# Moving the first block's rows to the scratch ring, the roots to the attention's banks, and spreading four weight sums

## The chip, the cores and the metric

The kernel runs on one core of one Trainium2 chip. The metric is the device time of one execution in microseconds (us). A core has five engines that this text names as the profile does: PE (TensorE, matmuls; PEld is its weight load), DVE (VectorE), ACT (ScalarE), POOL (GpSimd) and SP (SyncE, which here issues nearly all DMAs). Each works through its own queue of instructions, and they wait for one another by semaphores.

## The reference, cut to what matters

One layer of a streaming encoder over 2048 tokens of width 1024, with chunked softmax attention (16 heads of 64; a chunk of 64 frames reads itself and the 8 chunks before it) and a SwiGLU FFN of inner width 2816. Every sub-layer is normed before and after:

```python
def rms_norm(x, g):
    y = x * lax.rsqrt(jnp.mean(x * x, axis=-1, keepdims=True) + RMS_EPS)
    return y * g

h = rms_norm(x, g_pre_mix)
m = chunk_relpos_attention(h, w_qkv, w_o, rel_bias)   # softmax(q k / 8 + bias) v, then @ w_o
x = x + rms_norm(m, g_post_mix)
h = rms_norm(x, g_pre_ffn)
x = x + rms_norm((silu(h @ w_gate) * (h @ w_up)) @ w_down, g_post_ffn)
```

All of it is in float32. The kernel splits each factor of a dense product in a high and a low part and adds three products (`products`, lines 195 to 199; a triple of matmuls below).

## The kernel before, in words

The tokens lie along the free axis: a tile is 128 features by 512 tokens, and 8 such tiles (`KT`) make a quarter of the sequence (`NQ` = 4), two quarters a group (`NG` = 2). The work comes in four stages:

- `project()` (line 1320) makes values, queries and keys, group by group, and writes them to DRAM. The dense products go by a Strassen-like scheme of seven block products (`BLOCKS`, line 39) instead of eight, for which sums of four weight blocks, S1 to S4, are needed. `block_items` (line 894) builds them for group 0: it loads four raw blocks, and `make(n)`, called a few products ahead of the use of product n, splits the block for PE (ACT copies the high part, DVE subtracts for the low part, lines 130 to 132). After some of the products it calls `sum_`, which adds two raw blocks in place on DVE (line 905) and stores the sum by a DMA of POOL's queue (line 906), for group 1 to read. The values call it with `early=False`, the queries and keys (`w_qk`) and the gate and up weights (`w_gu`) with `early=True`.
- The attention runs in 128 slots of 128 queries (lines 1582 to 1610), eight pairs of heads for each of the quarters 1, 0, 2, 3 (`SEQ_OF`). In a slot PE transposes the probabilities (`transposed`, `fifth`), computes the scores of three slots ahead (`scores`), and every fourth slot multiplies by the values (`output`, whose high part is copied by ACT and whose low part by DVE in the function that it returns, `low`). PSUM banks: `ring` holds two banks, from slot 32 on three (`later_banks`), which the transposes and the output take in turn (`turn_of`, line 474); the scores have banks of their own; two banks of tag `mm` serve the rest.
- Beside a quarter of the attention runs the o-projection of the quarter before (`o_quarter`, line 609): eight output tiles of eight triples each, each tile in an `mm` bank, then copied by ACT to an `io` tile (lines 628, 629), stored to DRAM, and squared into the sum of its norm (line 631). `fill` (line 1552) hands out these triples over the slots, and for each of them `tick` gives one credit to the list `later`, whose steps run as their costs are covered.
- From the second of these quarters on (`n > 0`, line 1592) `later` holds the end of the quarter before: `Late.rows` turns the sum of squares into a row of roots (`rstd_steps`, line 267: eight small matmuls into a bank of `norm_bank`, a power on POOL, and after a pause four transposes into another such bank), `Late.write` norms the eight tiles, adds the residual on POOL and stores x1, and `Blocks.sums` (line 642) loads the eight tiles of x1 again, squares them on ACT, adds the squares on DVE into `total`, and takes the root for the norm before the FFN. `behind` (line 219) makes such a list of n loads and uses: step k issues load k and then use k - lag, and each step costs w n / (n + lag).
- The FFN: `gate_up` and `down`, group by group, on the same scheme of seven products.

Buffers that the change touches: the `io` ring of three tiles (line 249) holds the copies of the o-projection (`y`), the residuals of `Late.write` (`res`) and the rows of `Blocks.sums` (`sum`); the scratch ring (`scratch`, `narrow`, lines 238 to 247) has four tiles in the attention and holds the y tiles of `Late.write`, squares, and more in other stages. Only PE's order is written by hand (line 1531); the order of the instructions on the other engines and of SP's DMAs is made by the Tile scheduler when the program is built. All tiles of a ring are given out as they come free.

Of the kernel before, what the change touches and what calls it, by code (L numbers as in the profile page):

```python
# [13 lines left out]
ALU = mybir.AluOpType  # L14
# [9 lines left out]
KT = D // P  # L24
# [14 lines left out]
BLOCKS = ("B11", "B21", "T1", "T2", "B22", "T3", "T4")  # L39
# [10 lines left out]
def trunk(  # L50
# [14 lines left out]
    pe, act, dve, pool = nc.tensor, nc.scalar, nc.vector, nc.gpsimd  # L65
# [137 lines left out]
    later = deque()  # L203
# [15 lines left out]
    def behind(w, n, lag, load, use):  # L219


        def one(k):
            def go():
                if k < n:
                    load(k)
                if k >= lag:
                    use(k - lag)

            return w * n / (n + lag), go

        return [one(k) for k in range(n + lag)]

    def pause(w):
        return [(w, lambda: None)]
# [3 lines left out]
    def scratch(name):  # L238

        n = turn[0] % (4 + phase.get("tmp", 0))  # L240
        turn[0] += 1
        if n >= 4:
            return phase["fp"].tile([P, HALF], F32, tag="tmp", name=name, bufs=phase["tmp"])
        return xp.tile([P, HALF], F32, tag="sc", name=name, bufs=4)

    def narrow(name):
        return scratch(name)[:, :HALF]

    def io(name):
        return xp.tile([P, HALF], F32, tag="io", name=name, bufs=3)  # L250
# [4 lines left out]
    def nrm_tile(name):  # L255
        return row_tile("nrm", name)

    def add_square(src, total, first, eng=dve, sq=None):
        if first:
            act.activation(total, src, AF.Square)  # L260
            return
        if sq is None:
            sq = scratch("sq")[:, : src.shape[-1]]
        act.activation(sq, src, AF.Square)
        eng.tensor_tensor(total, total, sq, op=ALU.add)

    def rstd_steps(total, dst, wait=8.0, keep=None, bank=None, extra=None, then=None):

        nb = total.shape[-1] // P
        bank = bank or norm_bank
        r = {}

        def by_token():
            pt = bank("pssq")
            for b in range(nb):
                terms = [total] if extra is None else [total, extra]  # L280
                for n, t in enumerate(terms):
                    pe.matmul(
                        pt[:, 0, b : b + 1], t[:, b * P : b * P + P], ones[:, 0:1],
                        start=n == 0, stop=n == len(terms) - 1,
                    )
            m = const.tile([P, 4], F32, tag="ms", name="ms", bufs=2)
            dve.tensor_scalar(m[:, :nb], pt[:, 0, :nb], 1.0 / D, EPS, op0=ALU.mult, op1=ALU.add)  # L287
            r[0] = const.tile([P, 4], F32, tag="rs", name="rs", bufs=2) if keep is None else keep
            pool.tensor_tensor(r[0][:, :nb], m[:, :nb], neg_half.to_broadcast([P, nb]), op=ALU.pow)  # L289

        def back():
            if then is None:
                spread(r[0], dst, bank)
            else:
                then(transposed(r[0], nb, bank))

        return [(1.0, by_token)] + pause(wait) + [(1.0, back)]
# [39 lines left out]
        return [(w, f) for f in steps]  # L337

    def norm_bank(name):
        return ps.tile([P, 4, P], F32, tag="mm", name=name)  # L340

    def spread(r, dst, bank=norm_bank):
# [56 lines left out]
    phase = {}  # L399
# [45 lines left out]
    turn_of = [1]  # L445
    st_of, ring = [], []
# [11 lines left out]
    class Attend:  # L458
# [9 lines left out]
        def bank(self, name):  # L468

            if self.alone and name != "t5":  # L470
                return ps.tile([P, HALF], F32, tag="mm", name="tt")
            if self.alone:
                return ring[0]
            turn_of[0] += 1
            return ring[turn_of[0] % 3]
# [157 lines left out]
    class Blocks:  # L633
# [8 lines left out]
        def sums(self, w, on_all=False, which=range(2)):  # L642

            steps = []
            if on_all:
                self.rows = []
            for t in which:
                c = {}

                def load(k, t=t, c=c):  # L650
                    c[k] = io("sum")
                    sp.dma_start(c[k], self.src[t][:, k, :])

                def use(k, c=c):
                    if k == 0 and on_all:
                        self.total = phase["fp"].tile([P, HALF], F32, tag="tot", name="row", bufs=2)
                        self.rows.append(self.total)
                    elif k == 0:
                        self.total = nrm_tile("total")
                    add_square(c.pop(k), self.total, k == 0)  # L660

                steps += behind(w, KT, 2, load, use)
                if on_all:
                    steps.append((0.0, lambda t=t: later.extendleft(reversed(root_steps(self.rows[t], 1.5)))))
                    continue
                steps.append((5.0, lambda t=t: rstd_steps(self.total, None, keep=self.r[t])[0][1]()))
            return steps

        def spreads(self):
# [224 lines left out]
    def block_items(src, key, early=True, ahead=None):  # L894

        r = {}
        sums_d[key] = {a: dram.tile([P, 1024], F32, name=f"s_{key}_{a}") for a in ("S1", "S2", "S3", "S4")}

        def fetch_(names):
            for a in names:  # L900
                r[a] = phase["fp"].tile([P, 1024], F32, tag="w4", name="raw4", bufs=phase["w4"])
                sp.dma_start(r[a], src[BLOCK_AT[a]])

        def sum_(name, to, a, b, op=ALU.add):
            dve.tensor_tensor(r[to], r[a], r[b], op=op)
            last_pool[0] = pool.dma_start(sums_d[key][name], r[to])

        def make(n):
            w = w_tile(f"w{key}_{n}")
            a = FACTOR[n]  # L910
            split_part(*w, r[{"S1": "A21", "S2": "A11", "S4": "A12", "S3": "A21"}.get(a, a)])
            if n == ("B11" if early else "B21"):
                sum_("S1", "A21", "A21", "A22")
                sum_("S2", "A11", "A11", "A21")
            if n == "B21":
                sum_("S4", "A12", "A12", "A11")
            if n == "T2":
                sum_("S3", "A21", "A11", "A22", ALU.subtract)
            return w

        at = {"B11": ("A11", "A12"), "B21": ("A21", "A22")}
        if not early:
            at = {"B11": ("A11",), "B21": ("A12",), "T1": ("A21", "A22")}
        ahead = ahead or {}
        return [
            (lambda n=n: fetch_(at.get(n, ())), lambda _, n=n: make(n), *ahead.get(n, (6, 3))) for n in BLOCKS
        ]
# [227 lines left out]
    class Late:  # L1155
# [27 lines left out]

            return [(0.0, go)]

        def write(self, w, eng=dve):
            c = {}

            def load(dt):
                c[dt] = y, res = narrow("y"), io("res")  # L1190
                sp.dma_start(y, self.y[:, dt, :])
                sp.dma_start(res, self.res[:, dt, :])

            def use(dt):
                y, res = c.pop(dt)
                dve.scalar_tensor_tensor(
                    y, y, gt[:, self.gain, dt : dt + 1], self.total, op0=ALU.mult, op1=ALU.mult
                )
                eng.tensor_tensor(y, res, y, op=ALU.add)
                sp.dma_start(self.dst[:, dt, :], y)  # L1200

            return behind(w, KT, 2, load, use)


    rs, rows_of = [], {}
# [329 lines left out]
    sums_, done = weight_sums(), 0.0  # L1535
# [46 lines left out]
    for t in range(slots):  # L1582
        share = left[0] / max(per - t % per - 1, 1)
        if t > 0 and t % 4 == 0:
            fill(0.5 * share)
            low = jobs[t // 4 - 1].output()
            if t % per == 0:
                n = t // per - 1
                fill(1e9)
                drain()  # L1590
                work, left[0] = o_quarter(SEQ_OF[n]), KT * KT * 3 * C512
                if n > 0:
                    late = lates[SEQ_OF[n - 1]]
                    later.extend(late.rows(4.0) + late.write(3.0, pool))
                    later.extend(blocks[0].sums(2.0, which=[SEQ_OF[n - 1]]))
        if t == 16:
            fetch()
        elif t in (20, 22):
            part_split(t // 2 - 10)
        job = jobs[t // 4]  # L1600
        job.transposed(t % 4)
        if t + AHEAD - 1 < slots:
            jobs[(t + AHEAD - 1) // 4].scaled()
        ahead(t + AHEAD)
        if t > 0 and t % 4 == 0:
            low()
        fill(0.5 * share)
        job.fifth()
        if t % 4 < 3:
            fill(0.5 * share)  # L1610
# [96 lines left out]
```

## Time and profile before

| | |
|---|---|
| median of three runs | 2392.41 us (2391.65 to 2392.60) |
| the profiled execution | 2390.56 us, its span 2388.8 us |
| busy: PE, DVE, ACT, POOL | 98%, 68%, 48%, 13% of the span |
| first matmul of the o-projection's four quarters | 617.7, 729.4, 905.8, 1061.6 us |
| mean granted clock of TensorE | 0.993 |

The profile lists each instruction of the profiled execution with its start and duration, by line of the kernel. A tile's name stands before the arrow for what is written and behind it for what is read, as in `y<-mm`. In brackets stands the idle time of the engine before an instruction and what ended it. Matmuls overlap on PE, so the mean duration of one (about 0.39 us for 512 columns) is longer than the distance between two (0.22 us). The granted clock is 1 at full speed and 0.5 at half.

### The profile page before, as it was taken

The numbers are of one execution on the slowest core, as the hardware profiler recorded it, in microseconds if no ns is written. First come the engines' busy times: TensorE is split into PE (matmuls) and PEld (weight loads), VectorE is DVE, ScalarE is ACT, GpSimd is POOL, SyncE is SP. The second block draws the span as 40 slices with busy tenths as digits, with TensorE's granted clock in tenths as the row PEclk, the third lists the DMA queues.
The fourth block names the chain that finished last, engine by engine and source line by source line (L and its number), as shares of the span: only waits on it lengthen the run. The fifth ranks groups of instructions, "written<-read, shape, count | busy, mean of one in ns | idle before, by whom it ended". The sixth has DMA issues, their size and how long they took to land.

```text
span 2388.8 us, 32904 instructions
## 1 busy us (share of the span) xinstructions
PE 2330.5 (98%) x11456; PEld 1907.9 (80%) x11456; DVE 1635.1 (68%) x2618; ACT 1145.4 (48%) x2015; POOL 319.0 (13%) x422
## 2 busy tenths in 40 slices
PE   8999999989999989999999999999999999999998
PEld 6878788878777767778888888888888888888886
DVE  8776856666566666659777777687657676545577
ACT  6544543367666656656333332365443333334454
POOL 1021010034334434420000000000000000000001
PEclk9999999999999989999999999999999999999999
DMA  8799988688897988846776553577666657447664
GB/s 309 256 292 329 297 263 261 181 235 225 220 257 207 291 228 241 258 169 204 245 246 210 181 185 131 175 236 256 215 207 205 216 161 234 150 154 247 192 193 144
DMA packets 230358, 531.81 MB, mean 223 GB/s; under 512 B 26384, under 2 KB 42784, under 8 KB 225712
## 3 DMA queue, kind: packets, MB, share of 16 engines
q1 hardware_dynamic: 218288, 482.52, 63.8%
q0 software_dynamic: 11904, 47.19, 6.8%
q8 instruction: 90, 1.47, 0.2%
q14 instruction: 76, 0.62, 0.1%
HBM read 382.23 MB, written 170.44 MB: 231 GB/s over the span
## 4 chain that ended last, share of the span: by engine, by line
PE 68%; DVE 3%; ACT 1%; issue 1%; DMA 1%; POOL 0%; DVEq 0%; SPq 0%; ACTq 0%
PE pd L197 6%; PE pd L199 6%; PE pd L198 6%; PE pb L197 5%; PE pb L198 5%; PE pb L199 5%; PE tt L600 4%; PE pa L198 3%; PE pa L197 3%; PE pa L199 3%; PE pc L197 3%; PE pc L198 3%; PE pc L199 3%; PE tt L570 3%; PE mm L197 2%; PE mm L199 2%
## 5 line engine op out<-in xcount | busy, mean ns | idle before, releaser
L555 POOL TENSOR_SCALAR sc<-sc,rows 128x640 f32<-128x640 f32 (+4 forms) x256 | 194.5, 772 | 313.0 <-DVE rows L552 134.1
L543 ACT ACTIVATE sc<-sc,rows 128x640 f32<-128x640 f32 (+4 forms) x256 | 193.2, 757 | 72.5 <-DVE rows L539 71.4
L197 PE MATMUL pb<-hb,w_wg_T 128*128 128x512 f32 x528 | 206.0, 390 | 3.2 <-DVE terms L1012 3.2
L199 PE MATMUL pb<-hb,w_wg_T 128*128 128x512 f32 x528 | 205.5, 389 | 0.0
L198 PE MATMUL pb<-hb,w_wg_T 128*128 128x512 f32 x528 | 205.5, 389 | 0.0
L539 DVE CUSTOM_DVE_ANT_0 sc<-st,bias 128x640 f32<-128x640 f32 (+2 forms) x248 | 174.2, 734 | 39.7 <-PE st L531 26.0
L530 PE MATMUL st<-k,q 128*128 128x384 f32 (+3 forms) x432 | 139.2, 340 | 12.2 <-DVE rows L539 10.7
L573 DVE COPY pT<-tt 128x512 f32<-128x512 f32 (+3 forms) x128 | 81.6, 637 | 100.1 <-PE tt L570 64.9
L199 PE MATMUL pd<-a,w_d_T 128*128 128x512 f32 (+1 forms) x368 | 139.9, 380 | 0.1
L197 PE MATMUL pd<-a,w_d_T 128*128 128x512 f32 (+1 forms) x368 | 139.9, 380 | 0.0
L198 PE MATMUL pd<-a,w_d_T 128*128 128x512 f32 (+1 forms) x368 | 139.8, 380 | 0.0
L197 PE MATMUL pa<-hb,w_wg_B 128*128 128x512 f32 x352 | 136.9, 389 | 0.0
L198 PE MATMUL pa<-hb,w_wg_B 128*128 128x512 f32 x352 | 136.9, 389 | 0.0
L199 PE MATMUL pa<-hb,w_wg_B 128*128 128x512 f32 x352 | 136.9, 389 | 0.0
L570 PEld LDWEIGHTS tt<-ident,sc 128*128 128x128 f32 x928 | 107.1, 142 | 32.5 <-issue 15.3
L131 ACT ACTIVATE w_wg_T<-raw 128x1024 fp32r<-128x1024 f32 x88 | 93.0, 1057 | 79.7 <-PE pb L199 34.8
L570 PE MATMUL tt<-ident,sc 128*128 128x128 f32 x928 | 127.2, 277 | 0.7 <-ACT pT L575 0.3
L531 PE MATMUL st<-k,q 128*128 128x384 f32 (+3 forms) x432 | 126.3, 312 | 0.0
L354 DVE TENSOR_TENSOR a<-raw_a,a 128x512 fp32r<-128x512 f32 x154 | 105.8, 694 | 29.0 <-ACT a L353 28.7
L1014 ACT ACTIVATE terms<-terms 128x512 f32<-128x512 f32 x65 | 41.0, 631 | 172.0 <-DVE terms L1012 172.0
L132 DVE TENSOR_TENSOR w_wg_B<-raw,w_wg_B 128x1024 fp32r<-128x1024 f32 x66 | 80.7, 1222 | 62.0 <-ACT w_wg_B L131 62.0
L289 POOL TENSOR_TENSOR rs<-ms,neg_half 128x4 f32<-128x4 f32 (+1 forms) x7 | 7.5, 1066 | 857.2 <-DVE ms L287 857.2
(264 smaller groups left out, 6251.1 us busy)
## 6 DMA issues: line engine op xcount, KB each, us to landing
raw<-in_w_gu SPq DMA_DIRECT2D x77, 512.0 KB, 4.2
q<-q SPq DMA_DIRECT2D x62, 512.0 KB, 6.5
k<-k SPq DMA_DIRECT2D x54, 512.0 KB, 8.1
s_g_S<-raw POOLq DMA_DIRECT2D x44, 512.0 KB, 3.1
raw_d<-d_S SPq DMA_DIRECT2D x88, 256.0 KB, 3.8
raw_a<-aT SPq DMA_DIRECT2D x88, 256.0 KB, 3.7
raw<-s_g_S SPq DMA_DIRECT2D x44, 512.0 KB, 4.1
bias<-ext_d SPq DMA_DIRECT2D x124, 144.0 KB, 8.3
```

The lines of the kernel that those rows point to most:

```text
L131: act.activation(hi, raw, AF.Copy)
L197: pe.matmul(pt, a_hi, b_hi, start=first, stop=False, skip_group_check=go_on)
L198: pe.matmul(pt, a_hi, b_lo, start=False, stop=False, skip_group_check=go_on)
L199: pe.matmul(pt, a_lo, b_hi, start=False, stop=last, skip_group_check=go_on)
L354: eng.tensor_tensor(lo, src, hi.bitcast(F32), op=ALU.subtract)
L530: pe.matmul(st[:, a:b], q[:, 2 * h, cols], kk[:, h, key], start=True, stop=False)
L531: pe.matmul(st[:, a:b], q[:, 2 * h + 1, cols], kk[:, h, key], start=False, stop=True)
L539: dve.tensor_tensor_reduce(out=sc[:, :n], in0=st[:, c0 : c0 + n], in1=rev, scale=-1.0, scalar=3.0e38, op0=ALU.add, op1=ALU.min, accum_out= ...
L543: act.activation(sc[:, :n], sc[:, :n], AF.Exp, bias=nmax, scale=-1.0, accum_out=rows[:, h : h + 1])
L555: last_pool[0] = pool.tensor_scalar(sc[:, :n], sc[:, :n], rows[:, 2 + h : 3 + h], 1.0, op0=ALU.mult, op1=ALU.mult)
L570: pe.transpose(tt[:, u, :], sc[h][:, b * P : b * P + P], ident)
L600: pe.matmul(po[heads[h], c0:c1], v[:, kb, c : c + 64], self.pT[:, h, r, c0:c1], start=m == 0, stop=m == len(terms) - 1,)
```

## The change

- `norm_bank` gives a bank of the attention's ring while the attention runs, instead of an `mm` bank.
- `Blocks.sums` in the attention (`on_all` false) loads its rows to scratch tiles instead of `io` tiles, squares them in place instead of into another scratch tile, and uses a row one step after its load instead of two. The root comes 8 credits after the last of them instead of 5. In the FFN (`on_all` true) it stays as it was.
- `Late.write` in the attention uses its tiles one step after the load instead of two (`lag`); elsewhere it stays as it was.
- At a quarter's end the attention's last `low` is called ahead of the rest of the o-projection and of the new list, and the list begins with a pause of 5 credits.
- `block_items` makes one sum after each of four successive products. With `early`, before: S1 and S2 after B11, S4 after B21, S3 after T2; now S1 after B11, S2 after B21, S4 after T1, S3 after T2. Without: before S1, S2 and S4 after B21, S3 after T2; now S1 after B21, S2 after T1, S4 after T2, S3 after B22.

```diff
     def norm_bank(name):
+        if "psa" in phase:
+            turn_of[0] += 1
+            return ring[turn_of[0] % 3].rearrange("p (a b) -> p a b", a=4)
         return ps.tile([P, 4, P], F32, tag="mm", name=name)
...
                 def load(k, t=t, c=c):
-                    c[k] = io("sum")
+                    c[k] = io("sum") if on_all else narrow("sum")
                     sp.dma_start(c[k], self.src[t][:, k, :])
...
-                    add_square(c.pop(k), self.total, k == 0)
-
-                steps += behind(w, KT, 2, load, use)
+                    here = c.pop(k)
+                    add_square(here, self.total, k == 0, sq=None if on_all else here)
+
+                steps += behind(w, KT, 2 if on_all else 1, load, use)
...
-                steps.append((5.0, lambda t=t: rstd_steps(self.total, None, keep=self.r[t])[0][1]()))
+                steps.append((8.0, lambda t=t: rstd_steps(self.total, None, keep=self.r[t])[0][1]()))
...
-            if n == ("B11" if early else "B21"):
-                sum_("S1", "A21", "A21", "A22")
-                sum_("S2", "A11", "A11", "A21")
-            if n == "B21":
-                sum_("S4", "A12", "A12", "A11")
-            if n == "T2":
-                sum_("S3", "A21", "A11", "A22", ALU.subtract)
+            done = BLOCKS.index(n) - (not early)
+            if 0 <= done < 4:
+                sum_(*(
+                    ("S1", "A21", "A21", "A22"),
+                    ("S2", "A11", "A11", "A21"),
+                    ("S4", "A12", "A12", "A11"),
+                    ("S3", "A21", "A11", "A22", ALU.subtract),
+                )[done])
             return w
...
-        def write(self, w, eng=dve):
+        def write(self, w, eng=dve, lag=2):
...
-            return behind(w, KT, 2, load, use)
+            return behind(w, KT, lag, load, use)
...
             if t % per == 0:
+                low()
+                low = lambda: None
                 n = t // per - 1
...
-                    later.extend(late.rows(4.0) + late.write(3.0, pool))
+                    later.extend(pause(5.0) + late.rows(4.0) + late.write(3.0, pool, 1))
                     later.extend(blocks[0].sums(2.0, which=[SEQ_OF[n - 1]]))
```

## The prediction, made before the result was known

> **What bounds the kernel now.** I read the page first, then a table of stages, then who made PE wait, then the timeline around those waits. Of the page:
>
> ```profile
> span 2388.8 us, 32904 instructions
> PE 2330.5 (98%) x11456; PEld 1907.9 (80%) x11456; DVE 1635.1 (68%) x2618; ACT 1145.4 (48%) x2015; POOL 319.0 (13%) x422
> ```
>
> TensorE (PE) is busy for all but 58 us. The change takes away no matmul, so it can only give back idle time and time at a low clock. The stage table (busy us per engine, instructions, granted clock, DMA share) tells where these are. 729.4 to 905.8 and 905.8 to 1061.6 are the second and third quarter of the attention, in which the o-projection and the Late rows run beside it; I call them Q1 and Q2.
>
> ```profile
> core 0: us, PE busy (x) PEld busy (x) DVE busy (x) ACT busy (x) POOL busy (x), PEclk, DMA share, GB/s
> 0.00:58.00 58.00, 50.69 (x212) 40.11 (x213) 46.15 (x60) 39.31 (x60) 6.67 (x15) 0.94 0.85 310
> 58.00:120.00 62.00, 62.00 (x278) 51.08 (x277) 45.83 (x62) 36.81 (x56) 5.54 (x8) 1.00 0.75 257
> ...
> 729.40:905.80 176.40, 163.47 (x1046) 127.87 (x1045) 110.69 (x234) 107.84 (x236) 69.31 (x74) 0.96 0.84 244
> 905.80:1061.60 155.80, 151.69 (x988) 118.41 (x986) 95.46 (x207) 95.48 (x212) 60.97 (x68) 0.99 0.71 209
> ...
> 1240.00:1530.00 290.00, 286.81 (x1261) 236.18 (x1260) 212.34 (x271) 101.15 (x137) 14.41 (x27) 1.00 0.51 175
> ```
>
> Q1 idles 12.9 us, Q2 4.1, the first 58 us 7.3, the first FFN half 3.2. The clock below 1 comes from stretches at half speed, same columns:
>
> ```profile
> 844.47:851.30 6.83, 5.67 (x16) 3.02 (x18) 3.39 (x6) 2.15 (x5) 2.87 (x2) 0.50 0.75 204
> 861.53:868.36 6.83, 5.98 (x24) 5.61 (x25) 4.05 (x6) 3.08 (x4) 2.10 (x2) 0.50 1.01 198
> 1028.79:1032.20 3.41, 3.41 (x14) 3.01 (x13) 1.29 (x3) 1.73 (x3) 2.58 (x3) 0.50 0.01 6
> 35.50:38.90 3.40, 3.40 (x9) 2.63 (x10) 1.69 (x3) 2.89 (x5) 0.00 (x0) 0.50 0.24 67
> 52.60:56.00 3.40, 3.40 (x9) 2.63 (x9) 2.47 (x5) 3.18 (x5) 0.00 (x0) 0.50 0.91 302
> ```
>
> Each follows a PE wait. Work at half speed takes twice its time, so half of PE's busy time there is lost: 2.8 + 3.0 + 1.7 = 7.5 us in Q1 and Q2, 1.7 + 1.7 at the start. The waits of PE by name (total, times, longest):
>
> ```profile
> PE pssq L282 <- DVE total L265: 8.5, 2, 5.1
> PE mm L197 <- ACT sq L264: 5.8, 2, 5.3
> PE pb L197 <- DVE terms L1012: 3.2, 4, 1.6
> PE pb L197 <- DVE terms L1292: 2.9, 2, 2.2
> ```
>
> The first two belong to Q1 and Q2. The timeline shows how the second arises:
>
> ```profile
> 755.62 0.33 SPq L72 DMA_DIRECT2D res<-in_x  x1
> 759.28 0.33 SPq L72 DMA_DIRECT2D res<-in_x  x1
> 760.85 0.33 SPq L72 DMA_DIRECT2D res<-in_x  x1
> ...
> 766.82 0.40 PE L199 MATMUL mm<-hb,w 128*128 128x512 f32 x1
> ...
> 773.94 1.29 POOL L1199 TENSOR_TENSOR y<-res,y 128x512 f32<-128x512 f32 x1
> ...
> 785.92 0.59 ACT L629 ACTIVATE y<-mm 128x512 f32<-128x512 f32 x1
> ...
> 842.92 0.62 ACT L264 ACTIVATE sq<-sum 128x512 f32<-128x512 f32 x1
> ...
> 844.99 0.59 ACT L264 ACTIVATE sq<-mm 128x512 f32<-128x512 f32 x1
> ...
> 845.63 0.79 PE L197 MATMUL mm<-hb,w 128*128 128x512 f32 x1 [5.26 <-ACT sq L264]
> ```
>
> Three res loads fill the three io slots. The o-product that PE ends at 767.2 needs an io slot for its copy (line 628), and its copy starts at 785.92, 18.7 us later, behind the POOL addition that frees a slot. Later the sum rows take those slots: the square at 842.92 stands ahead of the dense square at 844.99, whose end frees a bank, and PE has waited 5.26 us for it.
>
> **The change part by part.** (1) *The io ring* (sums in scratch, write with lag 1). With lag 2 three loads are alive at once, with lag 1 two: of three io slots one stays for the copy, and during the sums all three. Scratch has four slots: two or three y tiles (one still storing) and the dense square, or two sums and that square, which fit since the sum is squared in place. This adds and removes no instruction; on SP the sums' loads now wait for a scratch slot instead of an io slot, and the q, k and bias loads of the pair two ahead stand behind them as before. The 5.26 us go.
>
> (2) *The root of the sums.* Its matmuls need total and, so far, an mm bank:
>
> ```profile
> 850.09 1.00 SPq L72 DMA_DIRECT2D sum<-x  x2
> ...
> 859.88 2.35 DVE L265 TENSOR_TENSOR total<-total,sq 128x512 f32<-128x512 f32 x2 [0.35 <-ACT sq L264]
> ...
> 862.38 0.56 PE L282 MATMUL pssq<-ones,total 128*128 128x1 f32 x2 [5.10 <-DVE total L265]
> ```
>
> The last two rows were loaded at 850, 12 us before the root. Now the root comes 8 credits after the last square instead of 5. A quarter hands out 64 credits (8 × 8 triples of matmuls), 2.4 us each in Q2's 155.8 us: 19 us of room instead of 12. Cost of the whole list: 5 + 6 + 24 + 16 + 8 = 59 of 64 (51 before), so nothing is left for the drain. I take the 8.5 us as gone, and with (1) the 7.5 us of clock: 5.3 + 8.5 + 7.5 = **21.3 us**.
>
> (3) *Lag 1 itself.* A sum is now used one step after its load: 2 × 8 / 9 = 1.78 credits, 4.3 us; a res row 2.67 credits, 6.5 us. Landing of sum loads in Q1 and Q2, then of res loads:
>
> ```profile
> DMA to landing us min/median/max: 2.8/5.8/10.1
> DMA to landing us min/median/max: 3.5/5.9/7.0
> ```
>
> The median sum is 1.5 us late, 16 times: 24 us of waiting on ACT, whose idle time in the sums' quarter of Q1 and Q2 (16 of 64 credits) is (68.6 + 60.3) / 4 = 32 us. What waits behind a square is Exp, the pT copies and the dense evictions. Exp is issued three slots (about 15 us) before its transposes, which covers single waits. Between 0 and 24 us I take **+3**, nearer the covered end. The Trainium skill, page "DMA: Bandwidth & Descriptors", section "Anatomy of one DMA — SWDGE (gpsimd) path", gives 2.0 us plus bytes / 436 GB/s for a DMA of the GpSimd path: by it, an estimate, 256 KB land in 2.6 us, lag 1 would cost nothing and the sum below would be 3 us lower. The least landing here is near that, the median is not; the measurement decides.
>
> (4) *Roots in the attention's ring.* Six norm banks (two for rows, one for sums, in Q1 and Q2) go to three tt banks. One is held about so long:
>
> ```profile
> 739.06 0.60 PE L349 MATMUL prs<-ident,rs 128*128 128x128 f32 x4
> ...
> 741.16 0.57 ACT L344 ACTIVATE osum<-prs 128x512 f32<-128x512 f32 x1
> ```
>
> From the transposes' end to the copy's end 2.1 us; a bank comes round after three turns, about a slot (5 us), two of whose turns lie together. Between 0 and 6 × 2.1 = 12.6 us I take **+1**. No gain beyond (1) and (2): what freeing mm gives is counted there.
>
> (5) *Four sums, one per product.* No DVE work goes; it is spread.
>
> ```profile
> L905 DVE TENSOR_TENSOR raw<-raw,raw 128x1024 f32<-128x1024 f32 x68 | 83.0, 1220 | 7.6 <-DMA raw<-in_w_qk 3.4 <-DMA raw<-in_w_gu 2.5 <-DMA x<-y 1.2
> L1012 DVE TENSOR_TENSOR terms<-pb,terms 128x512 f32<-128x512 f32 x86 | 58.8, 687 | 27.4 <-PE pb L199 27.4
> ```
>
> ```profile
> 18.48 2.48 DVE L905 TENSOR_TENSOR raw<-raw,raw 128x1024 f32<-128x1024 f32 x2
> 20.92 1.22 DVE L132 TENSOR_TENSOR w_wv_T<-raw,w_wv_T 128x1024 fp32r<-128x1024 f32 x1
> ...
> 29.07 1.22 DVE L905 TENSOR_TENSOR raw<-raw,raw 128x1024 f32<-128x1024 f32 x1
> ...
> 34.22 0.50 PE L197 MATMUL pv<-w_wv_T,hb 128*128 128x512 f32 x1 [1.45 <-ACT hb L694]
> ...
> 51.97 0.50 PE L197 MATMUL pv<-w_wv_T,hb 128*128 128x512 f32 x1 [2.25 <-ACT hb L353]
> ```
>
> At the start six sums run from 18.48 to 30.3, ahead of the activation parts that PE waits for; four of them (4.9 us) move behind product B21. By T2 only S3 (two, 2.4 us) has moved. Between 0 and the two waits with their clock (1.45 + 2.25 + 3.4 = 7.1) I take 3, since DVE is busy 80% here and gives back what it no longer does by T2. A query or gate product is 24 matmuls of 62.0 / 278 us, 5.35 us. DVE in a gate pair: under B22 four terms of 0.69, a split and two sums of 1.22, 6.4 us; under T3 five terms, split and sum, 5.9: 1.6 us behind when T4 wants the bank that T3's terms read. One sum less under B22 leaves 0.5. Of 3.2 us of L1012 I take 2, of 2.9 us of L1292 1.5: **6.5 us** in all, between 0 and 13. The stores of the sums wait on POOL's queue for DVE as before, one product later for some; behind them stand only the accumulating copies of the down weights, for which nothing waits before the FFN.
>
> (6) *The early lo split and the pause of 5.* No new instruction; the pause is covered by the 64 credits. If the split came ahead of a bias pass on DVE, that pass would be late by one term (0.69 us), three times; DVE idles 37% of Q1 and 39% of Q2, so **0**.
>
> Sum against the profiled execution (2390.56 us, its span 2388.8): 2390.6 - 21.3 + 3 + 1 - 6.5 = 2366.8. It lay 1.85 us under the median of the three runs (2392.41), so **2369 us**, own range 2358 (no cost in (3) and (4), (5) whole) to 2385 ((5) nothing, 10 us more in (3) and (4)).
>
> **Rivals.** *The place of the wait moves* (0.14). Only PE's order is written out (line 1531); the order on ACT, DVE and SP is planned from estimated times. If the copies keep their late places, or SP's loads, which wait in one line, stay late (DMA share 0.84 in Q1), another wait fills the 21.3 us and (5) alone remains: 2386 to 2392. Against it: Q2, with the same o-work, loses 5.8 us (4.1 and 1.7 of clock) where Q1 loses 18.7, so the flow of data does not force the wait.
>
> *Slower: lag 1 is too short* (0.10). Place: the squares on ACT. A waiting square holds the evictions and Exps behind it; the mm banks stay late, so the 21.3 us stay, and the 24 us of waiting reach PE: 2392.4 - 6.5 + 24 = 2410, or 2398 with half of them. It decides once landings pass 4.3 us by more than ACT's idle 2 us per step (32 us over 16); the longest, 10.1, does. For it, the median of 5.8; against it, a transposition that needs its Exp only 15 us later. The Trainium skill, "TensorE: Matmul & The Clock Gate", section "Architectural detail: the array is 16× 32×32, not 1× 128×128", calls the ACT and DVE queues strict FIFO; the eviction at 844.99 behind the square at 842.92 agrees.
>
> *More than the terms* (0.08): (3) and (4) cost nothing, (5) is whole, and the other 3.2 us of idle in Q1 and Q2 go too: about 2355.
>
> **How the numbers follow.** Forecast 0.68. The range, 2357 to 2392, leaves out the slower rival and the one beyond, 0.18. This kernel's measurement tells 0.2%, 4.8 us. Faster: 0.68 + 0.08 + 0.03 of the first rival = 0.79; the same 0.11; slower 0.10.
>
> **What would show it.** Right: no wait of mm L197 and pssq over 1 us in Q1 and Q2, evictions within about 5 us of their product, clock 1.00 in both, Q1 near 155 us; the first 58 us with less idle; no more than two of L905 between two of the weight splits at the start. Wrong: ACT idle before sq<-sum with a DMA as releaser, PE waiting for pssq or tt banks, or copies y<-mm still 15 us behind their products.

## The result and the profile after

The changed kernel takes 2388.89 us (median of 15 executions, 2383.23 to 2393.47) against 2394.03 us of the kernel before in the same comparison (15 executions, 2391.22 to 2402.25): a ratio of 0.9976, 95% interval 0.9966 to 0.9985. That is 5 us or 0.24% faster; 23 us were forecast. The sign is as predicted, the size is not.

The page of the changed kernel's profiled execution (2391.31 us; it lay above its median, as that of the kernel before lay below its own, so the two spans are nearly equal and stages are compared instead):

```profile
span 2389.3 us, 32876 instructions
PE 2331.4 (98%) x11456; PEld 1910.3 (80%) x11456; DVE 1635.3 (68%) x2618; ACT 1146.7 (48%) x2015; POOL 317.5 (13%) x422
```

Its table of stages, with columns as in the prediction; the last two rows are Q1 and Q2, cut at the first o-projection matmul of each quarter as before:

```profile
core 0: us, PE busy (x) PEld busy (x) DVE busy (x) ACT busy (x) POOL busy (x), PEclk, DMA share, GB/s
0.00:58.00 58.00, 51.62 (x227) 41.99 (x228) 48.99 (x65) 39.37 (x61) 6.73 (x15) 0.97 0.80 296
735.20:904.40 169.20, 160.13 (x1046) 125.56 (x1046) 107.82 (x232) 105.90 (x234) 65.47 (x74) 0.99 0.80 240
904.40:1064.80 160.40, 152.78 (x988) 118.58 (x987) 98.76 (x209) 97.94 (x214) 63.61 (x68) 0.99 0.72 217
```

Q1 fell from 176.4 to 169.2 us, Q2 rose from 155.8 to 160.4. The matmul counts are those of before (1046 and 988), so the sum of -2.6 us splits cleanly: PE's busy time, which holds the loss to the clock, fell by 3.3 in Q1 and rose by 1.1 in Q2; its idle time (window less busy) fell from 12.9 to 9.1 and rose from 4.1 to 7.6, which is -0.4 together. The waits of PE for mm and pssq in the two quarters were 14.3 us before (8.5 and 5.8 in the prediction's rows). Here are the waits of PE in the whole execution after, the longest lines first (us in total, times, longest):

```profile
PE st L533 <- DVE rows L542: 23.3, 22, 3.3
PE pv L197 <- ACT hb L356: 5.9, 3, 2.5
PE pb L197 <- DVE terms L1297: 5.3, 2, 3.2
...
PE pb L197 <- DVE terms L1017: 1.1, 2, 1.0
```

Neither mm nor pssq of the attention is in the list any more: the two waits that the prediction counted are gone. In their place stands the wait for the banks of the scores (line 533, which was line 530), freed by the score pass of DVE (line 542, which was 539). Of the 23.3 us these belong to Q1 and then to Q2, each the first line of the waits of that stretch:

```profile
PE st L533 <- DVE rows L542: 7.6, 5, 3.3
...
PE st L533 <- DVE rows L542: 5.6, 4, 2.0
```

The same two lines before, and then the line of the whole execution before:

```profile
PE st L530 <- DVE rows L539: 2.0, 3, 1.1
...
PE st L530 <- DVE rows L539: 0.6, 1, 0.6
...
PE st L530 <- DVE rows L539: 12.7, 16, 2.0
```

The last is the longest of PE's waits before, and the prediction's list of four lines leaves it out. Outside Q1 and Q2 this wait is 10.1 us in both kernels; all of its growth lies in these two quarters.

So 10.6 us of waits for scores arrived where 14.3 us of waits for mm and pssq left; two waits of 1.0 us for the transposes' bank make up most of the rest. The timeline around the longest of them:

```profile
799.28 0.80 DVE L542 CUSTOM_DVE_ANT_0 sc<-st,bias 128x640 f32<-128x640 f32 x1
799.36 1.27 POOL L1204 TENSOR_TENSOR y<-res,y 128x512 f32<-128x512 f32 x1 [1.82 <-DMA x<-y]
...
800.01 1.17 DVE L265 TENSOR_TENSOR osum<-osum,sq 128x512 f32<-128x512 f32 x1
...
800.60 2.44 POOL L558 TENSOR_SCALAR sc<-sc,rows 128x640 f32<-128x640 f32 x2
...
801.10 1.28 DVE L1201 SCALAR_TENSOR_TENSOR y<-y,gt,osum 128x512 f32<-128x512 f32 x1
...
802.30 0.81 DVE L542 CUSTOM_DVE_ANT_0 sc<-st,bias 128x640 f32<-128x640 f32 x1
...
803.18 0.52 PE L533 MATMUL st<-k,q 128*128 128x384 f32 x1 [3.26 <-DVE rows L542]
```

Between the score passes of the two heads of a pair (799.28 and 802.30) DVE runs a sum of squares and a norm term. Both heads share one tile of three score banks (line 458 of the changed kernel), and PE's next scores start at 803.18, when the second pass has ended (803.11). Two details are used below: the two terms took 1.17 and 1.28 us, where the shortest of their lines take 0.68 and 0.74, and GpSimd was at work meanwhile, adding a residual beside the first (until 800.63) and scaling the probabilities beside the second (line 558).

The evictions, which were to come within 5 us of their product, still do not:

```profile
774.52 0.60 ACT L632 ACTIVATE y<-mm 128x512 f32<-128x512 f32 x1 [1.22 <-PE mm L199]
...
781.17 0.33 SPq L72 DMA_DIRECT2D o<-y  x1
...
786.60 0.33 SPq L72 DMA_DIRECT2D res<-in_x  x1
786.71 0.40 PE L199 MATMUL mm<-hb,w 128*128 128x512 f32 x1
...
788.69 0.33 SPq L72 DMA_DIRECT2D res<-in_x  x1
...
796.24 1.29 POOL L1204 TENSOR_TENSOR y<-res,y 128x512 f32<-128x512 f32 x1 [6.08 <-DVE y L1201]
...
797.57 0.60 ACT L632 ACTIVATE y<-mm 128x512 f32<-128x512 f32 x1
```

The product that ends at 787.1 is copied at 797.57, just after a residual addition has ended (797.53) and directly behind other work of ACT. Two res loads still go out within 2.1 us of each other, lag 1 or not, and the copy made at 774.52 waited 6.6 us in line on SP before its store was even issued; the store landed at 789.3. From the third to the sixth tile of each quarter the squares start 11 to 18 us behind their products (before: 10 to 24), but this no longer makes PE wait for a bank.

### The profile page after: what moved, and what is told of

Its sections match the earlier page's. It is cut to its first block, busy times and chain, and to the rows that moved or that the text cites. A ratio compares the mean times of both kernels' runs of the same rounds, so it can differ in the third digit from the quotient of the medians.

```text
span 2389.3 us, 32876 instructions
## 1 busy us (share of the span) xinstructions
PE 2331.4 (98%) x11456; PEld 1910.3 (80%) x11456; DVE 1635.3 (68%) x2618; ACT 1146.7 (48%) x2015; POOL 317.5 (13%) x422
## 4 chain that ended last, share of the span: by engine, by line
PE 66%; DVE 3%; DMA 2%; ACT 1%; issue 1%; SPq 0%; POOL 0%; DVEq 0%; ACTq 0%
PE pd L199 6%; PE pd L197 6%; PE pd L198 6%; PE pb L197 5%; PE pb L199 5%; PE pb L198 5%; PE tt L603 3%; PE pa L199 3%; PE pa L197 3%; PE pa L198 3%; PE pc L197 3%; PE pc L199 3%; PE pc L198 3%; PE tt L573 2%; PE mm L199 2%; PE mm L197 2%
## 5 line engine op out<-in xcount | busy, mean ns | idle before, releaser
L533 PE MATMUL st<-k,q 128*128 128x384 f32 (+3 forms) x432 | 140.8, 343 | 24.9 <-DVE rows L542 21.3
L603 PE MATMUL tt<-pT,v 128*64 128x512 f32 (+3 forms) x832 | 119.9, 436 | 0.1
```

The costliest lines, as they stand in the source:

```text
L533: pe.matmul(st[:, a:b], q[:, 2 * h, cols], kk[:, h, key], start=True, stop=False)
L603: pe.matmul(po[heads[h], c0:c1], v[:, kb, c : c + 64], self.pT[:, h, r, c0:c1], start=m == 0, stop=m == len(terms) - 1,)
```

## The experiments

The theory after the result (**T**): the terms of the prediction were right in what they remove, but the lists of `later` now load DVE and ACT at other moments, and waits for the score banks take back most of it; which edits bring these waits can be found by undoing them one at a time. The rivals: **R1**, the waits went only because of the later root, and the rings do nothing; **R2**, lag 1 is too short; **R3**, the time is lost outside the attention; **R4**, the sums of the weights do the whole gain. Two executions of one kernel differ by up to 1.6 us in Q1 and 1.2 in Q2, and by several us in the projection of queries and keys (385.8 to 392.5 us over all), so single executions are compared by Q1 + Q2 and by the gate stage (first gate matmul to first down matmul), and totals only where many were made. All stage times here are worked out from the starts of those matmuls in the trace.

| kernel | Q1 | Q2 | Q1 + Q2 | gate stage |
|---|---|---|---|---|
| before / again | 176.4 / 175.6 | 155.8 / 156.0 | 332.2 / 331.6 | 427.0 / 427.9 |
| changed / again | 169.2 / 168.7 | 160.4 / 160.9 | 329.6 / 329.6 | 424.6 / 423.8 |
| four sums alone | 175.2 | 155.8 | 331.0 | 423.0 |
| all but the four sums | 169.1 | 162.0 | 331.1 | 430.6 |
| root at 8 and sums | 168.5 | 160.8 | 329.3 | 423.4 |
| pause of 5 and sums | 175.3 | 160.5 | 335.8 | 423.0 |
| root at 8, pause of 5 and sums | 168.7 | 161.5 | 330.2 | 423.1 |
| changed, neither pause nor root at 8 | 180.8 | 161.1 | 341.9 | 425.3 |
| changed, write at lag 2 | 168.0 | 155.6 | 323.6 | 425.2 |
| changed, roots in mm banks | 166.2 | 160.2 | 326.4 | 425.0 |
| changed, sums at lag 2 | 169.0 | 161.7 | 330.7 | 424.8 |
| changed, write at lag 2 and roots in mm banks / again | 166.8 / 165.2 | 157.4 / 157.8 | 324.2 / 323.0 | 424.2 / 423.1 |
| the same, additions on DVE / again | 165.1 / 165.1 | 156.0 / 154.8 | 321.1 / 319.9 | 423.5 / 424.7 |
| changed, pause of 7 | 173.0 | 154.5 | 327.5 | 424.2 |

**The two halves, and both kernels again.** The first kernel is the one before with only the new block of sums, the second the changed one with the old block:

```diff
-            if n == ("B11" if early else "B21"):
...
+            done = BLOCKS.index(n) - (not early)
```

> The kernel before with the four sums spread one per product, and nothing else of the change. Forecast's term (5): 6.5 us faster than the kernel before. Rival, read from the two traces: the start gains nothing by 80 us (5 us ahead at 41 us, lost again by 82), the queries end about 3 us later at 300 us and the FFN gives 2.3 us back, so within 2 us of the kernel before. With the project stage alone: the forecast has PE's first L530 score matmul earlier than before, the rival some 3 us later.

> The changed kernel with the sums of weight blocks back in their old places: rings, lags, roots, pauses alone. Forecast's terms (1) to (4): 17 us faster than the kernel before, both Q1 and Q2 near 155 us. Rival, read from the two traces: Q1 7 us shorter, Q2 5 us longer, so 2 to 3 us faster; PE waits for score banks (st) on DVE take the place of those for mm and pssq.

> The changed kernel unaltered, for a second trace. If the 5 us between the profiled executions' Q1 and Q2 and the medians are execution noise, Q1 and Q2 (169.2 and 160.4 us in the first trace) move by some us; if they are fixed by the order of the queues, they repeat within 1 us.

> The kernel before unaltered, for a second trace. Fixed order: Q1 176 and Q2 156 us again within 1 us, start and queries with the same waits. Noise: they move by some us.

Measured: the sums alone 0.9983 of the kernel before (0.9975 to 0.9992; 2390.86 us, 11 executions), all the rest alone 1.0008 (0.9999 to 1.0016; 2396.59 us, 12 executions); the changed kernel again 2384.45, the one before again 2395.44 us. The sums' 4 us lie in the gate stage. The stage of the kernel before, then of the sums alone:

```profile
0.00:96.50 96.50, 89.19 (x384) 71.74 (x385) 78.78 (x106) 63.05 (x95) 10.78 (x20) 0.96 0.75 272
1106.40:1533.40 427.00, 423.81 (x1877) 349.85 (x1877) 324.77 (x420) 155.68 (x213) 24.06 (x43) 1.00 0.55 190
```

```profile
0.00:97.00 97.00, 88.14 (x385) 71.54 (x386) 78.77 (x106) 62.44 (x95) 9.97 (x20) 0.96 0.76 278
1110.00:1533.00 423.00, 422.87 (x1877) 350.08 (x1877) 325.38 (x420) 156.29 (x213) 24.10 (x43) 1.00 0.55 192
```

The gate stage's 3.2 us of idle time fall to 0.1. At the start (first rows, until the first matmul of the queries) nothing is gained, since 7.3 us of idle become 8.9: PE's waits move from 31 to 52 us to 42 to 73 us. The attention's edits by themselves gave 0.5 to 1 us in the two quarters and a gate stage of 430.6 us, 3 longer, though they touch nothing there; the order that the scheduler makes changed for the whole program. So R4 holds for most of the total (4 of 5 us by medians, with intervals that overlap), and R3 for a part of it.

**The waits' own edits.** Two constants account for the root: its 8 credits and the pause of 5. The first kernel here is the changed one without either; the other three are the kernel before with the new sums and both, or one, of them.

```diff
-                    later.extend(pause(5.0) + late.rows(4.0) + late.write(3.0, pool, 1))
+                    later.extend(late.rows(4.0) + late.write(3.0, pool, 1))
...
-                steps.append((8.0, lambda t=t: rstd_steps(self.total, None, keep=self.r[t])[0][1]()))
+                steps.append((5.0, lambda t=t: rstd_steps(self.total, None, keep=self.r[t])[0][1]()))
```

> The changed kernel without the pause of 5 credits and with 5 instead of 8 credits before the root. Theory A (the pauses are covered and change only where things fall): Q1 169 and Q2 160 within 2 us. Rival (total is late without them): a wait for pssq on DVE total of 3 us or more in each.

> The kernel before with the four sums spread, the pause of 5 credits and the 8 credits before the root; io ring, lags, mm banks for the roots and the early lo split as before. Theory C (the delays are what the change lives on, the rings and lags add nothing or cost): the wait for pssq goes, Q1 165 to 170 and Q2 152 to 157 us, 9 to 14 us faster than the kernel before. Rival B (the io ring must be freed too): the wait for mm of 5.3 us in Q1 stays, Q1 over 170, and the time is that of the changed kernel or above.

> The kernel before with the four sums spread and 8 instead of 5 credits before the root of the sums, no pause. Theory C: total is then in time, no wait for pssq in either quarter; the wait for mm in Q1 stays, for the copies' places do not move: Q1 near 170, Q2 near 152. Rival: the mm bank is missing as well as total, and pssq waits 2 us or more in each.

> The kernel before with the four sums spread and the pause of 5 credits, the root 5 credits after the last square as before. Theory C, by the run without pauses (Q1 12 us longer than with both): the pause moves the loads of the Late rows against the bursts of the attention's loads, so Q1 and Q2 change by some us either way, while the waits for pssq on total stay at 3 to 5 us. Rival: the pause alone makes the waits go.

Measured: without them 2399.42 us, beside 2395.83 of the kernel before; both alone 0.9975 (0.9965 to 0.9986; 2387.47 us, 7 executions), as much as the whole change; root at 8 alone 2386.78 us, pause alone 2395.27 us. The waits in Q1 of the changed kernel without either:

```profile
PE tt L282 <- DVE total L265: 5.5, 1, 5.5
PE st L533 <- DVE rows L542: 4.8, 4, 1.9
PE mm L197 <- ACT sq L264: 4.1, 1, 4.1
```

of the kernel with the root at 8 alone, in Q1 and then in Q2:

```profile
PE mm L197 <- ACT sq L264: 5.8, 2, 5.3
PE st L530 <- DVE rows L539: 1.8, 2, 1.1
...
PE st L530 <- DVE rows L539: 3.7, 1, 3.7
PE tt L584 <- DVE hb L607: 1.7, 1, 1.7
PE pssq L282 <- DVE total L265: 1.7, 1, 1.7
```

and of the kernel with both, in Q1:

```profile
PE st L530 <- DVE rows L539: 4.1, 3, 2.2
PE mm L197 <- ACT sq L264: 3.1, 1, 3.1
```

Without the two constants the root's wait is back, 5.5 us in Q1 and 5.0 in Q2 (now for a tt bank, where the root sits). With the 8 credits alone it is gone in Q1 and halved in Q2, from 3.4 to 1.7 us; with both constants it is gone in both. So the later root removes it, as term (2) says, though the 8 credits by themselves do not remove all of it. The pause alone leaves it (4.9 us in Q1, 4.5 in Q2), and its two quarters are 3.6 to 4.8 us longer than those of the kernels before it and of the sums alone; the pause is worth its place only beside the later root, if at all. The mm wait stays at 3.1 us in Q1 and 2.2 in Q2 with both constants and the old rings, and at 4.1 us in Q1 with the new rings and neither constant. Where both stand together it is gone, so the constants do not end it by themselves, and neither do the rings. Of the attention's other edits the scratch ring and the early `low` are left as what it takes, since undoing each of the others (below) brings back 1.4 us at most; no run tries these two apart. The end of this wait is also no gain that Q1 shows: with the root at 8 alone Q1 is 168.5 us, as short as in the changed kernel, and 5.8 us of waits for mm are still in it. The two quarters stand at 330 us with or without the rings, so R1 holds for the net effect as the change was written.

**Undoing the rest, one at a time.** Rows written two steps behind their load; roots in mm banks; sums two steps behind:

```diff
-late.write(3.0, pool, 1)
+late.write(3.0, pool)
...
-        if "psa" in phase:
-            turn_of[0] += 1
-            return ring[turn_of[0] % 3].rearrange("p (a b) -> p a b", a=4)
...
-                steps += behind(w, KT, 2 if on_all else 1, load, use)
+                steps += behind(w, KT, 2, load, use)
```

> The changed kernel with Late.write used two steps after its load again, all else as changed. Theory A (lag 1 brings the norms L1201 so close to the landing that they stand between the two score passes of DVE and PE waits for st): the st waits at 62 to 90 us into Q1 and Q2 (4 to 5 us each with their clock) go, Q1 near 164 and Q2 near 156 us. Rival B (the io ring needs lag 1): three res tiles fill io again, copies y<-mm lag 15 to 20 us as before, a wait for mm returns; Q1 over 172, Q2 over 160.

> The changed kernel with the roots' banks taken from mm again, all else as changed. Theory A: the waits for tt at 24 us of Q1 and Q2 (1.0 us each, behind the copies L588) come from the extra turns of the ring and go; but with dense squares 18 us late in the sums' stretch the mm banks are full when the root comes, so a wait for pssq of 3 to 5 us returns in each: Q1 near 172, Q2 near 164. Rival: the pause of 8 credits is enough and the mm bank is free by then: Q1 and Q2 1 us shorter than changed, 168 and 159.

> The changed kernel with the sums' rows used two steps after the load, still in scratch and squared in place. Theory A (scratch is the ring that holds the dense squares back now): three rows in scratch make the squares sq<-mm later than 18 us and PE waits for mm 3 us or more; Q1 near 173, Q2 near 164. Rival (lag 1 costs waits for landing on ACT): the st waits at 114 to 138 us of Q1 (3.6 us) and 116 of Q2 go and both are 2 to 4 us shorter.

Measured: 2385.72, 2384.52 and 2393.75 us, one execution each. By the stages, lag 2 of the write gives back 6 us, nearly all in Q2; the roots in mm banks 3 us, in Q1; the lag of the sums nothing. The row of Q2 of the first, then that of Q1 of the second:

```profile
902.50:1058.10 155.60, 150.68 (x988) 117.23 (x986) 98.59 (x209) 97.93 (x214) 61.41 (x68) 1.00 0.76 224
```

```profile
731.30:897.50 166.20, 158.78 (x1046) 124.20 (x1046) 107.50 (x232) 106.01 (x234) 68.46 (x74) 1.00 0.83 244
```

Q2 is back at the 155.8 us of before, with no clock lost; its waits for scores fall from 5.6 to 3.7 us.

**Both undone, twice.**

> The changed kernel with Late.write at lag 2 and the roots' banks from mm, the two parts whose undoing shortened Q1 or Q2. If the two gains add (Q1 169 - 1 - 2.5, Q2 160.5 - 5 - 0.5): Q1 165.5, Q2 155, 8 to 9 us less than the changed kernel, 2380 to 2382 us, ratio to the kernel before near 0.994. If they do not, since full mm banks meet the root (dense squares 18 to 21 us late): a wait for pssq or mm of 2 us or more, and no gain over the changed kernel.

> The changed kernel with its rows written two products late again and without the roots in the attention's ring. If the short wait for the rows and the roots in the ring really cost the quarters some 2 and 5 us, the time is again near 0.995 of the kernel before (0.994 to 0.996), Q1 near 166 and Q2 near 157. If the first look was a lucky execution: 0.997, as the change.

Measured: 0.995 of the kernel before (0.9938 to 0.9962; 2382.09 us, 6 executions), and on another chip 0.9937 (0.9925 to 0.995; 2378.84 us, 5 executions). Both intervals lie under that of the changed kernel. Against the kernel with the two constants and the sums alone, which differs from it by the scratch ring for the sums (with their lag) and the early `low`, the two quarters are 6 to 7 us shorter: this is what these two bring where the write has lag 2, and with lag 1 of the write it is lost again. The two undone together give no more than lag 2 alone (323.6 against 323.0 to 324.2), so the roots' 3 us are lost only beside lag 1. Of R2 the price is near (the prediction's +3 for lag 1 was 2 to 6), its mechanism does not hold: the sums' loads, whose landing it was about, are indifferent to their lag, and ACT waited only 2.4 us for them in Q1 and Q2 of the changed kernel. Nor does the landing of the write's own rows explain it: DVE waited for them 0.9 us in Q2 of the changed kernel, but 2.0 us in the shortest Q2 of the table, that of the pause of 7. One rival is left. Lag 1 makes nine steps of 2.67 credits out of ten of 2.4 and so moves every step of the write; whether the short distance or the moved steps bring the waits, no run tells apart.

**What stretches DVE's terms.** In the timeline above two terms took 1.7 times their usual time beside GpSimd's instructions. The next kernel is the last one with the residual additions on DVE (twice); in the third the values' sums S3 and S4 go to GpSimd instead:

```diff
-late.write(3.0, pool)
+late.write(3.0)
...
-            dve.tensor_tensor(r[to], r[a], r[b], op=op)
+            (dve if early or name in ("S1", "S2") else pool).tensor_tensor(r[to], r[a], r[b], op=op)
```

> The kernel of lag 2 with mm roots (Q1 166.8, Q2 157.4 us), with the residual additions of Late.write in the attention on DVE instead of POOL. Theory D (the waits for st at 69 us into both quarters come from DVE terms that are stretched, 1.22 to 2.0 and 0.68 to 1.8 us, while POOL's additions run): the stretched terms fall back to 1.22 and 0.69 where no L555 runs, the wait at 69 falls under 1 us, Q1 + Q2 from 324 to 320 us or less, though DVE gets 16 x 0.69 = 11 us more work. Rival (DVE has simply too much between two score passes): one more term per tile there, waits of 2 to 4 us stay or grow, Q1 + Q2 324 to 332.

> The same, with the residual additions on VectorE instead of GpSimd. If VectorE's terms with two inputs in SBUF are stretched by GpSimd's additions, and the score banks wait for that, Q1 and Q2 together are 2 to 3 us shorter than in the kernel beside it, and the time 0.1% below it. If VectorE only has 11 us more to do: the same time or 1 to 4 us more.

> The kernel of lag 2 with mm roots, with S3 and S4 of the two value weights added on POOL instead of DVE (four additions of 128x1024). Theory E (spreading gave the start nothing since DVE is full there and the same work is due a product later): 4.9 us less on DVE shorten the stage to the first query matmul from 96.4 to 92 to 94 us. Rival F (the waits there are for ACT and for landings, or POOL's reads stretch DVE's terms as much): 96 to 98 us.

Measured: 2378.24 us (one execution) and 0.9927 of the kernel before (0.9914 to 0.9941; 2377.57 us, 5 executions), the best here; with the sums on GpSimd 2387.82 us, the stage of the values (until the first matmul of the queries) 104.3 us long where the others' is 95 to 98, its quarters, 165.2 and 157.4 us, as without that edit. The low split of the weights (line 132) in Q1 and Q2 in the changed kernel (ns, least, median and longest):

```profile
L132 DVE TENSOR_TENSOR w<-raw,w x16: 1209/1221/1941, 757.8 to 1049.2; 128x1024 fp32r<-128x1024 f32 x16
```

and with the additions on DVE:

```profile
L132 DVE TENSOR_TENSOR w<-raw,w x16: 1206/1220/1258, 754.3 to 1035.9; 128x1024 fp32r<-128x1024 f32 x16
```

The stretching of this term goes when the additions leave GpSimd: in the changed kernel its three longest (1.66 to 1.94 us) lay beside additions, two of 1.51 us beside the scaling of the probabilities. That of the norm term (line 1201, now 1198) goes in part: its longest was 1.75 us, beside an addition, and is 1.28 us with the additions on DVE, beside that scaling, which stays on GpSimd. The line in the changed kernel and then with the move:

```profile
L1201 DVE SCALAR_TENSOR_TENSOR y<-y,gt,osum x16: 740/748/1754, 773.5 to 1017.4; 128x512 f32<-128x512 f32 x16
...
L1198 DVE SCALAR_TENSOR_TENSOR y<-y,gt,osum x16: 739/742/1282, 770.4 to 983.6; 128x512 f32<-128x512 f32 x16
```

Q1 and Q2 in the second executions, first without and then with the move:

```profile
729.90:895.10 165.20, 158.42 (x1046) 124.06 (x1045) 108.06 (x232) 106.12 (x234) 67.37 (x74) 1.00 0.84 245
895.10:1052.90 157.80, 151.77 (x988) 118.58 (x987) 99.35 (x209) 97.22 (x214) 62.87 (x68) 0.99 0.74 222
```

```profile
731.70:896.80 165.10, 158.70 (x1046) 124.22 (x1046) 110.23 (x240) 106.03 (x234) 57.70 (x66) 1.00 0.84 246
896.80:1051.60 154.80, 150.68 (x987) 117.16 (x985) 101.90 (x217) 97.21 (x214) 51.75 (x60) 1.00 0.75 225
```

DVE took over 16 additions (8 more instructions in each row), yet its busy time grew by only 4.7 us in both together, where 16 at 0.68 us are 10.9. Q2 is 3 us shorter, Q1 the same; of the waits for scores, 6.6 us in Q1 and 5.8 in Q2 without the move, 5.9 and 3.4 are left. In the totals the difference is 1.3 us by medians of five, and the intervals overlap: the stretching beside the additions is shown, its worth in time is not settled beyond these 1 to 3 us.

**A longer pause.** The changed kernel with `pause(7.0)`:

> The changed kernel with a pause of 7 credits instead of 5, nothing else. Theory G (Q1 and Q2 hang on where the planned order happens to put DVE's terms between the two score passes, so any shift moves them): Q1 or Q2 differs by 2 us or more from 169 and 160.5, with the st waits at other places. Rival (they are set by rings and lags): both within 1 us.

Measured: 2390.15 us, Q1 3.8 us longer and Q2 5.9 us shorter. In Q1 stands

```profile
PE tt L282 <- DVE total L265: 7.1, 1, 7.1
```

and Q2 has 1.3 us of waits for scores left. In Q1 the root again comes ahead of its sums, now with a tt bank, though it keeps its 8 credits: the load of the last row goes out only at 878.5 us, 11 us before the root can run. In Q2 a shift by 2 credits takes away 4.3 of 5.6 us of waits for scores without removing any work. So these waits depend on when the steps fall, not only on how much DVE has to do.

## Why the prediction was wrong

Point by point:

- **(1) The io ring, 5.3 us.** The mm wait went, as forecast, but only with the constants and the rings together, and Q1 was as short with the wait still in it (168.5 us). The step "with lag 1 two: of three io slots one stays for the copy" did not bring the copies forward: a slot stayed with the copy before until its store, which stood in SP's line, had landed, 15 us after that copy. The reading of the cause was weak too. In the trace before, the last addition that read one of those three res tiles is the one at 773.94, over at 775.23, and the copy came 10.7 us later, directly behind another instruction of ACT. At that time the copy's place in ACT's queue held it, not a full io ring; whether the ring had set that place when the order was planned is not shown.
- **(2) The root, 8.5 us.** Right in mechanism; both pssq waits are gone. The later root is what ended them, by its 8 credits in Q1 and with the help of the pause in Q2; a pause of 7 brought a wait of 7.1 us back.
- **The clock, 7.5 us.** It was forecast to return with the waits. Q1 got back 3.3 us of busy time and Q2 lost 1.1, since the new waits bring stretches at half speed as well (0.99 in both quarters).
- **"I take the 8.5 us as gone, and with (1) the 7.5 us of clock".** This is the step that failed. It took the idle time of a wait for a gain, and did not ask what is late next. The waits for score banks were in the profile before, the longest line of PE's waits (12.7 us) and 2.0 and 0.6 us in Q1 and Q2; the prediction named neither. In Q1 and Q2 they came to 7.6 and 5.6. Of 21.3 us the two quarters kept 2.6, costs (3) and (4) included, and most of the 5 us in the total is term (5). That is the first rival, at 0.14 too cheap. The argument against it ("the flow of data does not force the wait") was beside the point: as far as the timeline and the run with the pause of 7 show, the new wait is one of order on DVE, not of data.
- **(3) Lag 1, +3.** For the sums 0, for the rows 2 to 3 (with the roots in mm banks) or 6 us (as written). Both lie in the range given; the reason given, the landing of the sums, is not what cost it. By the figure of the Trainium skill, "DMA: Bandwidth & Descriptors", "Anatomy of one DMA — SWDGE (gpsimd) path", 256 KB land in 2.6 us, an estimate for DMAs of the GpSimd path. In the trace of the changed kernel these loads, which are SP's, took longer: the sums landed after 2.7 to 9.0 us with a median of 6.5, the res rows after 3.2 to 9.3 with a median of 6.3.
- **(4) Roots in the attention's ring, +1.** Nothing beside lag 2, 3 beside lag 1.
- **(5) The four sums, -6.5.** The gate's share was 2 and measured 4; the start's was 3 and measured nothing, as other waits of PE for the activation parts took its place; the queries' 1.5 cannot be told from their scatter of 4 us (the wait of 2.9 us that it was taken from is 5.1 us in the second execution of the same kernel). The total of 4 us is about what the whole change brought.
- **(6) The early `low` and the pause, 0.** The pause is not free: with the sums alone it makes the two quarters 4.8 us longer. The early `low` was not tried by itself.

With lag 1 of the write and the roots in the ring undone, the rest of the change comes to 0.50 to 0.63% (13 to 15 us by medians), and Q1 and Q2 together are 7 to 9 us shorter than before: a part of what was argued for was there, and parts of the change hid it. Even then 12.3 us of waits for scores are left in the two quarters. What stays open is why Q2 is 5 us longer in some of these kernels (with lag 1 of the write as the change has it, with the root at 8 credits alone, with the pause of 5 alone) and not in others (with lag 2 in its place, or with lag 1 and the pause of 7). The runs show these edits moving the waits, not by which instruction.

## What to carry to other kernels

A wait that a change removes is a gain only after the next buffer of the same engine has been checked: list the engine's shorter waits in that stage, and ask what the moved steps put in front of them. Where several edits go in together, undo them one at a time on top of the whole; here the four sums and two constants gave as much as the whole change, undoing one shortened lag gave 6 us, and each looked harmless by itself. Where a scheduler makes the order, small waits wander from edit to edit, so the price of a part is to be read from stages that repeat within 1 or 2 us, not from the total.

## What the runs showed of the hardware

VectorE instructions with two inputs in SBUF took longer beside some of GpSimd's instructions: beside a residual addition up to 1.94 us for the low split that takes 1.21 alone and 1.75 for the norm term of 0.74, and beside the scaling of the probabilities 1.51 for the low split and 1.28 for the norm term. The score pass, with one of its inputs in PSUM, stays at 0.80 and 0.81 us in the same stretch. The Trainium skill, "SBUF — State Buffer", "Who interferes with whom", says that a VectorE instruction with two SBUF inputs contends with a GpSimd instruction that reads SBUF. The trace agrees: without a GpSimd instruction beside them the low splits of Q1 and Q2 take 1.21 to 1.22 us and the norm terms 0.74 to 0.75, and the low split falls back to at most 1.26 when the additions move to VectorE. Not every overlap stretches as much: with the additions moved, the low splits beside the scaling took 1.21 to 1.26 us. Which engine holds the other up, and for how long, these runs do not show.
